# Queries and keys of a decoder layer projected transposed, split where they are made, and loaded whole by the attention

## The chip, the cores and the metric

The kernel runs on one core of a Trainium2 chip. The core has a matrix engine (TensorE, PE in the profile; its weight loads are PEld), a vector engine (VectorE, DVE), an activation engine (ScalarE, ACT), a general engine (GpSimd, POOL), a queue processor (SyncE, SP), and 16 DMA engines between the device memory and the on-chip memory SBUF. TensorE writes to PSUM, 8 banks of 128 x 512 f32. The metric is the device time of one execution in microseconds (us), the median of three.

## The reference

One step of a hybrid decoder layer, for a prompt of 1024 rows of width 1024 and for 8 samples with 8192 cached positions each. All data is f32. Cut to what matters here:

```python
xn = rmsnorm(x, g_mix)                       # x * rsqrt(mean(x*x) + eps) * g
h = xn @ w_in                                # columns: q 512 | k 512 | v 512 | f 8 | u 512 | z 512
logf = log_sigmoid(h_f + b_f); u = gelu(h_u); z = rmsnorm(gelu(h_z), g_sgu_v)
c = cumsum(logf)                             # forget gates, per head
s = q @ k.T / 8 + c[query] - c[key]          # 8 heads of 64, causal
att = softmax(s) @ v
sgu = u * (causal(w_s) @ z + b_s)            # in chunks of 128 rows
x = x + concat(rmsnorm(att), rmsnorm(sgu)) @ w_o
x = x + cross_attention(x, memory); x = x + conv_ffn(x); y = rmsnorm(x)
```

The samples go through the same layer with paged caches of keys, values and gates. The outputs include y and the prompt's k, v and logf.

## The kernel before

**Precision.** A product of two f32 matrices is made of three matmuls in the engine's faster f32r type: each operand is split into a high part (ACT copies it to f32r) and the residual (DVE subtracts), and `gemm3` (L238) sums high x high, high x low, low x high. `split` (L209) makes the parts, `wload` (L221) loads a weight block and splits it (L212, L213).

**Projections (`p1`, L302).** x comes transposed (`xT`), is multiplied by the norm's gain and split into 16 tiles `xh`, `xl` that stay for all of `p1` (`load_x`, L314). The row factor 1/rms(x) is applied after the matmul. The sums of squares come from x in its row layout: `stats` (L323) loads it once more in 4 MB, 1 MB at a time into the `kv` buffers, and ACT squares and sums (L207); these loads are put behind those of `xT` in SP's queue. Then five column blocks follow: Q, F with U, K, V, Z, each a weight load (`loaded`, L346) and 8 row tiles of 24 matmuls. A row tile lies in PSUM with rows on partitions; `evac` (L382) multiplies by the row factor on ACT and ACT's queue stores it row-major (q_d, o_k, o_v). `by_rows` (L387) runs four tiles at once, weight block by weight block. `gate_rows` (L439) makes the cumulated gates and their residuals and stores them in cq_d and ck_d, with rows of ones beside them.

**Attention (`attention`, L629).** It runs for half 0 (rows 0 to 511, 4 key tiles) and half 1 (8 key tiles), in each over 4 pairs of heads. `load` fetches q, k and v of a pair; `setup` (L646) transposes q and k on TensorE (L649, L672), ACT copies the high parts (L655, L656, L676, L680; in half 1 POOL makes one of the copies, L678), DVE the residuals (L657, L681), and POOL's queue adds the gate rows (L658, L667). The results are the operands of `scores` (L684): queries' high and residual parts stacked over 128 partitions against keys' high parts twice (L696), and queries' high parts with 4 gate rows against keys' residuals with 4 gate rows (L698). Row maximum on DVE (L701), exponential on ACT (L706), transposes (`turn`, L724), products with v (`values`, L740). `LD` and `ST` say at which step of a pair the next one's load and setup are written down.

**Beside it.** `pmem` (L590: the memory's keys and values) and `gating` (L535: the spatial gating of one half) are generators that `mix` (L1550) weaves into the attention of half 0 and the cross-attention: each `yield` gives a weight, and the other side runs until the weights balance. `early` (L1581) starts the attention and `pmem` within Z. The samples' step (`decode`, L1123) is woven into everything by `PACE`: gathers of 1 MB of cache by POOL's queue into four `kv` buffers (L1175, L1236), multiplies on DVE or POOL (L1183), sums on DVE (L1187), matmuls with the values (L1242).

**Buffers.** Large tiles `U`: 18 of 128 x 1024 f32. Small tiles `T2`: 7 of 128 x 520. Weight buffers `WRAW`: 4, `kv`: 4. PSUM: 6 banks in turn for most products (`BK`, L128), one `MS`, one `DV`. The order of instructions on each engine is made ahead of time by a list scheduler, which takes the written order as priority.

Of the kernel before, what the change touches and what calls it, by code (L numbers as in the profile page):

```python
# [18 lines left out]
P = 128  # L19
# [39 lines left out]
KP = 2  # L59
PW = 1  # L60
LD = [(0, 1, 0), (0, 0, 0)]
ST = [(0, 1, 1), (0, 1, 1)]
# [12 lines left out]
SB = 2  # L75
# [8 lines left out]
def build(nc, tc, ctx, a, phases=None):  # L84
# [97 lines left out]
    q_d = dram.tile([T, AW], F32, tag="q_d", name="q_d")  # L182
    k_d, v_d = a["o_k"], a["o_v"]
# [3 lines left out]
    cq_d = dram.tile([NH, 4, T], F32, tag="cq_d", name="cq_d")  # L187
    ck_d = dram.tile([NH, 4, T], F32, tag="ck_d", name="ck_d")
# [108 lines left out]
    def newest(e):  # L297

        return next(i for i in reversed(nc.cur_bb.bb.instructions) if i.engine == e)


    def p1(early):  # L302
        rstd = const.tile([P, 8], F32, tag="rstd", name="rstd")
        rstd8 = const.tile([P, 8], F32, tag="rstd8", name="rstd8")
        ssx = sm([P, 8], "ssx", 1)
# [6 lines left out]
        xh, xl = [[U([P, T], F32R) for _ in range(8)] for _ in range(2)]  # L312

        def load_x(kk, hf):  # L314

            raw = WRAW(1024).rearrange("p (k t) -> p k t", t=512)
            c = slice(hf * 512, hf * 512 + 512)
            nc.sync.dma_start(raw, a["xT"][kk * 256 : (kk + 1) * 256, c].rearrange("(k p) t -> p k t", p=P))
            for q in range(2):
                k = kk * 2 + q  # L320
                split(raw[:, q, :], xh[k][:, c], xl[k][:, c], scale=gp[:, G_MIX + k : G_MIX + k + 1])

        def stats(hf):  # L323
            for q in range(2):
                xr = KV().rearrange("p (c d) -> p c d", d=D)
                t0 = hf * 4 + q * 2
                with tc.issue_after(x_in):
                    nc.sync.dma_start(xr, a["x"][t0 * P : (t0 + 2) * P, :].rearrange("(c p) d -> p c d", p=P))
                for i in range(2):
                    ssq_into(ssx[:, t0 + i : t0 + i + 1], xr[:, i, :])  # L330
            c = slice(hf * 4, hf * 4 + 4)
            r = rstd_of(ssx[:, c], D, 4, "r4")
            nc.vector.tensor_copy(rstd[:, c], r)
            nc.vector.tensor_scalar(rstd8[:, c], r, 0.125, None, op0=ALU.mult)
# [11 lines left out]
        def loaded(c0, n, parts, first=False):  # L346

            sp = [(BK(), off, m) for off, m in parts]
            ws = []
            for kk in range(4):  # L350
                if first:
                    load_x(kk, 0)
                w_ = wload(wpair(a["w_in"], kk, c0, n), 2 * n)
                for ps, off, m in sp:
                    sample_mm(ps, w_[2], kk, xsT, m, off)
                ws.append(w_)
                if first and kk == 1:
                    constants()
            return ws, [(ps, m) for ps, off, m in sp]


        ws, sps = loaded(O_Q, 512, [(0, 512)], first=True)
        for kk in range(4):
            load_x(kk, 1)
        x_in = newest(ENG.SP)
# [9 lines left out]
        stats(0)  # L375
        stats(1)
# [5 lines left out]
        def evac(ps, dst, sc, tt):  # L382
            t = T2()
            nc.scalar.activation(t, ps, AF.Copy, scale=sc[:, tt : tt + 1])
            nc.scalar.dma_start(dst[tt * P : (tt + 1) * P, :], t)

# [13 lines left out]
        pss = yield from by_rows(0, ws)  # L400
        for tt in range(8):
            ps = BK() if tt > 3 else pss[tt]
            if tt > 3:
                mm_chunk(tt, ws, ps, 0, 512)
                yield 5.2
            evac(ps, q_d, rstd8, tt)
# [32 lines left out]
        def gate_rows():  # L439
# [3 lines left out]
            for hf in range(2):  # L443
# [11 lines left out]
                for r_, src in ((0, ch), (1, cl)):  # L455
                    nc.sync.dma_start(cq_d[:, r_, s], src.bitcast(F32))
                    nc.sync.dma_start(cq_d[:, 2 + r_, s], one)
                    nc.sync.dma_start(ck_d[:, r_, s], one)
                    ng = T2()[:8]
                    nc.vector.tensor_scalar(ng, src.bitcast(F32), -1.0, None, op0=ALU.mult)  # L460
                    nc.sync.dma_start(ck_d[:, 2 + r_, s], ng)


        for c0, dst in ((O_K, k_d), (O_V, v_d)):
            ws, sps = loaded(c0, 512, [(0, 512)])
            for tt in range(8):
                ps = BK()
                mm_chunk(tt, ws, ps, 0, 512)
# [14 lines left out]
                evac(ps, dst, rstd, tt)  # L483
# [51 lines left out]
    def gating(hf):  # L535
# [6 lines left out]
        for pr_ in range(2):  # L542
            z = U([P, 2, 512])
            u = U([P, 2, 512])
# [3 lines left out]
            nc.sync.dma_start(u, sgu_d[rows, :].rearrange("(c p) d -> p c d", p=P))  # L548
            for i in range(2):
# [3 lines left out]
            yield 1  # L553
# [36 lines left out]
    def pmem():  # L590
        rm = const.tile([P, 2], F32, tag="rm", name="rm")
        ssm = sm([P, 2], "ssm", 1)
        for mt in range(2):
            t = U([P, D])
            nc.sync.dma_start(t, a["mem"][mt * P : (mt + 1) * P, :])
            ssq_into(ssm[:, mt : mt + 1], t)
        r = rstd_of(ssm, D, 2, "r2")
        nc.vector.tensor_copy(rm, r)
        mh, ml = [], []
        for q in range(2):  # L600
            h, l = U([P, 4, 256], F32R), U([P, 4, 256], F32R)
            raw = WRAW(1024).rearrange("p (k m) -> p k m", m=256)
            nc.sync.dma_start(raw, a["memT"][q * 512 : (q + 1) * 512, :].rearrange("(k p) m -> p k m", p=P))
            for k in range(4):
                kk = q * 4 + k
                split(raw[:, k, :], h[:, k, :], l[:, k, :], scale=gp[:, G_MEM + kk : G_MEM + kk + 1])
            mh.append(h)
            ml.append(l)
        yield 0.1
# [19 lines left out]
    def attention(hf, late=None, at=3):  # L629
# [3 lines left out]
        def load(hp):  # L633
            cs = slice(hp * P, (hp + 1) * P)
            qn = T2().rearrange("p (i c) -> p i c", c=P)
            nc.sync.dma_start(qn, q_d[hf * 512 : (hf + 1) * 512, cs].rearrange("(i p) c -> p i c", p=P))
            if hf == 0:
                kvn = U([P, 2 * nk, P])
                kn, vn = kvn[:, :nk, :], kvn[:, nk:, :]
            else:  # L640
                kn, vn = U([P, nk, P]), U([P, nk, P])
            nc.sync.dma_start(kn, k_d[: nk * P, cs].rearrange("(i p) c -> p i c", p=P))
            nc.sync.dma_start(vn, v_d[: nk * P, cs].rearrange("(i p) c -> p i c", p=P))
            return qn, kn, vn

        def setup(hp, qn, kn, vn):  # L646
            tr = (MS, BB, BA)[SB]()
            for i in range(4):
                nc.tensor.transpose(tr[:, i * P : (i + 1) * P], qn[:, i, :], ident)  # L649
            qab, ka, kb = [], [], []  # L650
            for j in range(2):
                h = hp * 2 + j
                rows = slice(64 * j, 64 * j + 64)
                qq = U([P, 2, 512], F32R)
                nc.scalar.activation(qq[0:64, 0, :], tr[rows, :], AF.Copy)  # L655
                nc.scalar.activation(qq[0:64, 1, :], tr[rows, :], AF.Copy)  # L656
                nc.vector.tensor_tensor(qq[64:128, 0, :], tr[rows, :], qq[0:64, 0, :].bitcast(F32), op=ALU.subtract)  # L657
                nc.gpsimd.dma_start(qq[64:68, 1, :], cq_d[h, :, hf * 512 : (hf + 1) * 512])  # L658
                qab.append(qq)
                if hf == 0:  # L660
                    kab = U([P, 2, 512], F32R)
                    ka.append(kab[:, 0, :])
                    kb.append(kab[:, 1, :])
                else:
                    ka.append(U([P, nk * P], F32R))
                    kb.append(U([P, nk * P], F32R))
                nc.gpsimd.dma_start(kb[j][64:68, :], ck_d[h, :, : nk * P])  # L667
            for kh in range(hf + 1):
                yield
                tr = (MS, BB, BA)[SB]()  # L670
                for i in range(4):
                    nc.tensor.transpose(tr[:, i * P : (i + 1) * P], kn[:, kh * 4 + i, :], ident)  # L672
                s = slice(kh * 512, kh * 512 + 512)
                for j in range(2):
                    rows = slice(64 * j, 64 * j + 64)
                    nc.scalar.activation(ka[j][0:64, s], tr[rows, :], AF.Copy)  # L676
                    if KP & 1 << hf:
                        nc.gpsimd.tensor_copy(ka[j][64:128, s], ka[j][0:64, s].bitcast(F32))  # L678
                    else:
                        nc.scalar.activation(ka[j][64:128, s], tr[rows, :], AF.Copy)  # L680
                    nc.vector.tensor_tensor(kb[j][0:64, s], tr[rows, :], ka[j][0:64, s].bitcast(F32), op=ALU.subtract)  # L681
            got.append((qab, ka, kb, vn))

        def scores(qkv, ls, blk, j, ii):  # L684
# [9 lines left out]
            for ch in range(nch):  # L694
                s = BA()[:, :n]
                mmul(s, qab[j][:, 0, i * P : (i + 1) * P], ka[j][:, ch * n : ch * n + n], start=True, stop=False)  # L696
                diag = ch == nch - 1
                mmul(s, qab[j][0:68, 1, i * P : (i + 1) * P], kb[j][0:68, ch * n : ch * n + n], start=False, stop=not diag)  # L698
# [75 lines left out]
        got = []  # L774
        for _ in setup(0, *load(0)):
            pass
        nxt = None
        yield 2
        for hp in range(4):
            for _ in nxt or ():  # L780
                pass
            qkv, nxt = got.pop(), None
            if hp == at and late:
                late()
            for blk in range(2):
# [5 lines left out]
                for j in range(2):  # L791
                    for ii in range(2):
# [20 lines left out]
                        if hp < 3 and (blk, j, ii) == ST[hf]:  # L813
                            nxt = setup(hp + 1, *raw)
                        if nxt:
                            next(nxt, None)
                            yield 1
# [838 lines left out]
    "o_y": (T, D), "o_ys": (NB, D), "o_k": (T, AW), "o_v": (T, AW), "o_lf": (T, NH), "o_mk": (NMEM, D), "o_mv": (NMEM, D),  # L1656
# [81 lines left out]
```

## Time and profile before

| | us |
|---|---|
| median of 3 runs (1969.85 to 1985.79) | 1971.17 |
| the profiled execution | 1971.44 |
| its span, first to last instruction | 1969.6 |
| TensorE busy in it | 1828.8 (93%) |
| DVE, ACT, POOL busy in it | 1395.3, 730.1, 538.0 |

DMA moved 517.05 MB at a mean of 263 GB/s. A line of a timeline reads: start, duration, engine, line of the kernel, operation, output <- input, shapes, and in brackets the idle time of the engine just before and what ended it. In a table of windows each engine has its busy time and, in brackets, its instructions; then come the granted TensorE clock, the share of the DMA engines' time and GB/s. A line of waits reads: who waited <- for whom, us in total, times, longest. Ends of matmuls are modelled, so overlapping matmuls each show more than their distance.

### The profile page before, as it was taken

The page shows a single profiled execution, that of the slowest core. Times are in us where ns is not written, and L with a number is a line of the kernel's source. Part 1 is how long each engine was busy: PE and PEld are TensorE (multiplying, and loading weights), DVE is VectorE, ACT ScalarE, POOL GpSimd, SP SyncE. Part 2 cuts the span into 40 slices and gives each one's busy share as a digit, 9 for nine tenths or more (in the row PEclk, how much of TensorE's full clock was granted, in tenths as well). Part 3 has the DMA queues.
Part 4 walks back from the last instruction along what each step waited for, and adds up shares of the span by engine and source line. Part 5 has one row for each costly group of instructions (what it writes and reads, how often), then busy time and mean ns, then how long its engine had stood idle before and what let it go on. Part 6 is the DMA issues. An engine that isn't in the chain of part 4 may idle for free.

```text
span 1969.6 us, 23939 instructions
## 1 busy us (share of the span) xinstructions
PE 1828.8 (93%) x9159; PEld 1295.1 (66%) x9159; DVE 1395.3 (71%) x1651; ACT 730.1 (37%) x1344; POOL 538.0 (27%) x376
## 2 busy tenths in 40 slices
PE   8899989878899789699999999998999999999997
PEld 5777766556666547477777776666567677667773
DVE  4877466786767798898989999988335549653442
ACT  5332246566723232332432332433324333242331
POOL 1664342342245433323234243333110000000000
PEclk9999989989999989899999999999999999999998
DMA  8766777654487898788778798989664458665755
GB/s 327 257 242 211 290 303 244 244 166 142 161 342 275 325 335 324 249 324 299 291 268 336 271 356 339 374 314 363 232 217 151 150 188 273 233 220 211 271 192 193
DMA packets 160466, 517.05 MB, mean 263 GB/s; under 512 B 20168, under 2 KB 41928, under 8 KB 127584
## 3 DMA queue, kind: packets, MB, share of 16 engines
q0 software_dynamic: 38528, 270.88, 36.5%
q1 hardware_dynamic: 114912, 232.06, 33.8%
q10 hardware_dynamic: 6912, 12.59, 1.7%
q8 instruction: 72, 1.18, 0.2%
q14 instruction: 42, 0.34, 0.0%
HBM read 493.63 MB, written 21.84 MB: 262 GB/s over the span
## 4 chain that ended last, share of the span: by engine, by line
PE 71%; DVE 10%; DMA 9%; issue 5%; ACT 3%; POOL 1%; SPq 0%; ACTq 0%; DVEq 0%; POOLq 0%
PE ba L242 12%; PE ba L243 12%; PE ba L244 12%; PE bb L242 6%; PE bb L243 5%; PE bb L244 5%; PE dv L1242 5%; DVE s L1187 2%; DMA wr<-w_in 2%; DVE kv L1183 2%; DMA kv<-cache_k,kidx 2%; DVE wl L213 1%; PE dv L1485 1%; DMA u<-zg_d 1%; PE ba L1014 1%
## 5 line engine op out<-in xcount | busy, mean ns | idle before, releaser
L212 ACT ACTIVATE wh<-wr 128x1024 fp32r<-128x1024 f32 (+2 forms) x220 | 228.9, 1044 | 506.7 <-PE ba L243 176.5
L213 DVE TENSOR_TENSOR wl<-wr,wh 128x1024 fp32r<-128x1024 f32 (+2 forms) x220 | 268.5, 1231 | 176.7 <-PE ba L244 70.1
L1187 DVE TENSOR_REDUCE s<-kv 128x32 f32<-128x2048 f32 (+1 forms) x139 | 292.1, 2107 | 18.0 <-POOL kv L1183 17.4
L1175 POOL DMA_INDIRECT kv<-cache_k,kidx x128 | 174.3, 1362 | 449.1 <-PE dv L1242 208.4
L1236 POOL DMA_INDIRECT kv<-cache_v,kidx x128 | 182.5, 1426 | 354.3 <-PE dv L1242 224.7
L242 PE MATMUL ba<-wh,u 128*128 128x512 f32 (+1 forms) x674 | 262.4, 391 | 5.5 <-ACT u L212 2.8
L1183 DVE TENSOR_TENSOR kv<-kv,d 128x2048 f32<-128x2048 f32 (+1 forms) x109 | 248.2, 2282 | 24.8 <-DMA kv<-cache_k,kidx 23.7
L243 PE MATMUL ba<-wl,u 128*128 128x512 f32 (+1 forms) x674 | 258.7, 384 | 3.0 <-DVE wl L213 3.0
L244 PE MATMUL ba<-wh,u 128*128 128x512 f32 (+1 forms) x674 | 255.8, 383 | 0.2 <-DVE u L213 0.2
L242 PE MATMUL ba<-u,wh 128*128 128x512 f32 x568 | 227.4, 401 | 0.0
L244 PE MATMUL ba<-u,wl 128*128 128x512 f32 x568 | 225.9, 398 | 0.0
L243 PE MATMUL ba<-u,wh 128*128 128x512 f32 x568 | 225.1, 397 | 0.0
L242 PEld LDWEIGHTS ba<-wh,u 128*128 128x128 f32 x674 | 128.4, 190 | 54.0 <-issue 18.7
L243 PEld LDWEIGHTS ba<-wl,u 128*128 128x128 f32 x674 | 128.1, 190 | 33.9 <-issue 7.1
L244 PEld LDWEIGHTS ba<-wh,u 128*128 128x128 f32 x674 | 127.6, 189 | 28.9 <-issue 3.4
L1242 PE MATMUL dv<-kv,s 128*32 128x512 f32 x1024 | 135.2, 618 | 2.5 <-DMA kv<-cache_v,kidx 2.2
L1183 POOL TENSOR_TENSOR kv<-kv,d 128x2048 f32<-128x2048 f32 (+1 forms) x30 | 119.3, 3985 | 53.5 <-DMA kv<-cache_k,kidx 47.8
L242 PEld LDWEIGHTS ba<-u,wh 128*128 128x128 f32 x568 | 107.3, 189 | 40.4 <-issue 10.1
L244 PEld LDWEIGHTS ba<-u,wl 128*128 128x128 f32 x568 | 107.0, 188 | 34.5 <-issue 10.9
L243 PEld LDWEIGHTS ba<-u,wh 128*128 128x128 f32 x568 | 107.2, 189 | 33.3 <-issue 9.2
L242 PE MATMUL bb<-wh,u 128*128 128x512 f32 (+1 forms) x318 | 124.3, 391 | 1.6 <-ACT u L212 0.9
L243 PE MATMUL bb<-wl,u 128*128 128x512 f32 (+1 forms) x318 | 122.7, 386 | 1.0 <-DVE wl L213 1.0
(394 smaller groups left out, 2947.7 us busy)
## 6 DMA issues: line engine op xcount, KB each, us to landing
wr<-w_up SPq DMA_DIRECT2D x88, 512.0 KB
kv<-w_up SPq DMA_DIRECT2D x22, 1024.0 KB
wr<-w_down SPq DMA_DIRECT2D x40, 512.0 KB
kv<-w_down SPq DMA_DIRECT2D x11, 1024.0 KB
wr<-w_in SPq DMA_DIRECT2D x16, 512.0 KB
wr<-w_o SPq DMA_DIRECT2D x16, 512.0 KB
wr<-w_cq SPq DMA_DIRECT2D x16, 512.0 KB
wr<-w_co SPq DMA_DIRECT2D x16, 512.0 KB
```

The source lines that it names most:

```text
L212: nc.scalar.activation(h, src, AF.Copy)
L213: nc.vector.tensor_tensor(l, src, h.bitcast(F32), op=ALU.subtract)
L242: mmul(out, sh, mh, start=(i == 0), stop=False)
L243: mmul(out, sh, ml, start=False, stop=False)
L244: mmul(out, sl, mh, start=False, stop=(i == n - 1))
L1014: mmul(ps, mv[:, mt, dd * P : (dd + 1) * P], pT[:, mt, :], start=(mt == 0), stop=(mt == 1))
L1175: nc.gpsimd.indirect_dma_start(kv, None, a["cache_k"], off(kidx[:, b, ch : ch + 1]))
L1183: eng.tensor_tensor(kvv[:, i : i + m, :], kvv[:, i : i + m, :], qb.unsqueeze(1).broadcast_to((P, m, 512)), op=ALU.mult)
L1187: nc.vector.tensor_reduce(s[:, ch * 4 + i : ch * 4 + i + m, :].rearrange("p k h -> p (k h)"), kvv[:, i : i + m, :].rearrange("p k (h d) -> ...
L1236: nc.gpsimd.indirect_dma_start(kv, None, a["cache_v"], off(kidx[:, b, ch : ch + 1]))
L1242: mmul(dv[32 * j : 32 * j + 32, :], s[:, ch * 4 : ch * 4 + 4, :].rearrange("p k h -> p (k h)"), kvv[:, j, :], start=(ch == 0), stop=(ch == ...
L1485: mmul(ps[32 * j : 32 * j + 32, q * 256 : (q + 1) * 256].rearrange("p (f c) -> p f c", f=2), xsT[:, k, :], rv[:, k], start=(k < 4), stop=( ...
```

## The change

The queries and keys are projected with the operands exchanged, so that heads lie on partitions and rows on columns; there the row factor, laid out as a row block `rrow`, is multiplied in, the split is made, and the parts are stored as the attention needs them. The attention loads these operands whole; its transposes, copies and residuals are gone. The output k is stored transposed and turned on the host after the run. The sums of squares are made from `xT`: ACT squares, TensorE sums over partitions. `pmem` loads ahead, `gating` waits longer between load and use, and for half 0 uses weight buffers. The core of it:

```diff
+    q1_d, k1_d = (dram.tile([NH, P, T], F32, tag=n_, name=n_) for n_ in ("q1_d", "k1_d"))
+    q2_d, k2_d = (dram.tile([NH, 68, T], F32, tag=n_, name=n_) for n_ in ("q2_d", "k2_d"))
...
+        rrow = U([P, 2, 512])
-        def stats(hf):
...
+        def squares(kk, raw):
             for q in range(2):
+                x2 = T2()
+                nc.scalar.activation(x2, raw[:, q, :], AF.Square)
+                x2s.append((kk * 2 + q, x2))
+        def squares_in():
+            for k, x2 in x2s:
+                j = k % 4
+                mmul(sums[-1][32 * j : 32 * j + 32, :], ones[:, 0:32], x2, start=(k < 4), stop=(k >= 4), tile_position=(0, 32 * j))
+            x2s.clear()
+        def sums_out():
+            t = T2()
+            nc.scalar.activation(t, sums.pop(), AF.Copy)
+            sums_sb.append(t)
+        def factors(hf):
+            t = sums_sb.pop()
+            ps = MS()
+            for i in range(4):
+                mmul(ps[:, i : i + 1], t[:, i * P : (i + 1) * P], ones[:, 0:1], start=True, stop=True)
+            r = rstd_of(ps[:, 0:4], 32 * D, 4, "r4")
+            nc.vector.tensor_copy(rstd[:, hf * 4 : hf * 4 + 4], r)
+        def row_factors(hf):
...
+            mmul(ps, ones, dg, start=True, stop=True)
+            nc.scalar.activation(rrow[:, hf, :], ps, AF.Copy)
...
+        def evac_T(ps, hf, hp, scale, to1, to2, out=None):
+            c = slice(hf * 512, hf * 512 + 512)
+            t, h, l = T2(), T2(512, F32R), T2(512, F32R)
+            nc.vector.scalar_tensor_tensor(t, ps, scale, rrow[:, hf, :], op0=ALU.mult, op1=ALU.mult)
+            split(t, h, l)
+            x, y = (l, h) if out is None else (h, l)
+            heads = lambda dst, r0: dst[2 * hp : 2 * hp + 2, r0 : r0 + 64, c]
+            nc.scalar.dma_start(heads(to1, 0), h.bitcast(F32))
+            nc.scalar.dma_start(heads(to1, 64), x.bitcast(F32))
+            nc.scalar.dma_start(heads(to2, 0), y.bitcast(F32))
+            if out is not None:
+                nc.sync.dma_start(out[hp * P : (hp + 1) * P, c], t)
...
+        pss = yield from by_cols(0, ws, {
+                0: [squares_in, sums_out, partial(second, 0)],
+                1: [partial(second, 1)],
+                2: [partial(factors, 0)],
+                3: [squares_in],
+                4: [partial(second, 2)],
+                5: [partial(row_factors, 0), partial(second, 3)],
+                7: [squares_in, sums_out],
+            })
...
@@ gating
+            z, u = (U([P, 2, 512]) if hf else WRAW(1024).rearrange("p (c d) -> p c d", d=512) for _ in range(2))
...
+            yield 6
...
-            yield 1
+            yield 3
@@ attention
+            q1, q2 = U([P, 2, 512], F32R), U([P, 2, 512], F32R)
+            nc.sync.dma_start(q1.bitcast(F32), q1_d[heads, :, qc].rearrange("h p t -> p h t"))
...
+                for j in range(2):
+                    nc.sync.dma_start(ka[j].bitcast(F32), k1_d[hp * 2 + j, :, kc])
+                    nc.sync.dma_start(kb[j][0:68].bitcast(F32), k2_d[hp * 2 + j, :, kc])
+            nc.sync.dma_start(q2[0:68].bitcast(F32), q2_d[heads, :, qc].rearrange("h p t -> p h t"))
+            vn = (T2() if hf == 0 else U([P, nk * P])).rearrange("p (i c) -> p i c", c=P)
-        def setup(hp, qn, kn, vn):
...
```

`by_cols` is `by_rows` with the operands exchanged, for the four pairs of heads of half 0; the other tiles follow one by one. `second` is `load_x` and `squares` for half 1.

More of the change, by code (lines that the diff above doesn't have):

```diff
@@ L74 @@
 LT = 3
-SB = 2
 KS = 2
@@ L356, in loaded @@
                 ws.append(w_)
+                if first:
+                    squares_in()
+                    squares(*x_)
                 if first and kk == 1:
@@ L772, in drain @@
                 queue.pop(0)()
[L774 to L777, printed above, removed]
+        raw = load(0)
         yield 2
         for hp in range(4):
[L780 to L782 removed]
+            qkv = raw
             if hp == at and late:
```

205 lines of the change are left out of this document (103 added, 102 removed).

## The prediction

> **What bounds the kernel now.** I read the page's busy times first, then a table of windows by stage, then the timeline around the widest hole that it shows, and last the waits and the chain of the two attentions. The table's rows are, in order: the projections Q (to 59.3 us), F with U (to 121), K (to 167), V (to 221), Z (to 276.5), the attention of half 0 (to 396), of half 1 (to 528.6), merge, output projection and cross-attention of half 0 (to 820), and the rest. Its columns are TensorE (PE), its weight loads, VectorE (DVE), ScalarE (ACT), GpSimd (POOL), granted clock, DMA.
>
> ```profile
> span 1969.6 us, 23939 instructions
> PE 1828.8 (93%) x9159; PEld 1295.1 (66%) x9159; DVE 1395.3 (71%) x1651; ACT 730.1 (37%) x1344; POOL 538.0 (27%) x376
> ```
>
> The table by stage:
>
> ```profile
> 0.00:59.30 59.30, 52.03 (x210) 37.28 (x210) 24.00 (x57) 35.56 (x52) 8.18 (x13) 1.00 0.90 327
> 59.30:121.00 61.70, 55.58 (x442) 50.12 (x442) 55.02 (x32) 19.29 (x30) 48.59 (x17) 0.94 0.67 242
> 121.00:167.00 46.00, 42.25 (x181) 32.52 (x180) 37.12 (x33) 11.47 (x18) 20.48 (x9) 0.96 0.66 233
> 167.00:221.00 54.00, 54.00 (x248) 39.93 (x247) 29.52 (x21) 14.66 (x18) 21.42 (x12) 1.00 0.65 229
> 221.00:276.50 55.50, 55.50 (x267) 38.75 (x266) 30.92 (x22) 17.21 (x29) 25.15 (x16) 1.00 0.73 275
> 276.50:396.00 119.50, 98.64 (x520) 71.12 (x520) 79.79 (x138) 71.38 (x160) 42.75 (x38) 0.89 0.76 269
> 396.00:528.60 132.60, 110.00 (x715) 76.66 (x711) 95.61 (x205) 89.14 (x244) 41.73 (x47) 0.93 0.43 144
> ```
>
> TensorE is the bound: 1828.8 of 1969.6 us. V and Z have no hole at all. The attentions lose 119.5 - 98.6 = 20.9 and 132.6 - 110.0 = 22.6 us, and there the clock column falls most, to 0.89 and 0.93. So whatever moves off TensorE or out of its way in the attentions can be gained, and whatever is put into the projections is paid unless it fits beside the matmuls.
>
> ```profile
> 276.96 0.60 PE L672 MATMUL ba<-cp,u 128*128 128x128 f32 x4
> ...
> 281.37 1.06 ACT L212 ACTIVATE wh<-wr 128x1024 fp32r<-128x1024 f32 x1 [3.95 <-DMA wr<-w_ck]
> 282.33 0.57 ACT L655 ACTIVATE u<-ba 64x512 fp32r<-64x512 f32 x1
> ...
> 284.50 0.68 DVE L681 TENSOR_TENSOR u<-ba,u 64x512 fp32r<-64x512 f32 x1 [0.40 <-ACT u L680]
> ...
> 284.52 0.47 PE L696 MATMUL ba<-u,u 128*128 128x128 f32 x1 [6.96 <-ACT u L680]
> ```
>
> Here half 0's attention begins. TensorE has transposed the first queries and keys at 276.3 to 277.6 and has nothing until 284.52: the copies that build its operands (L655, L676, L680) stand on ACT behind a weight split that waits for w_ck. After it the matmuls start 0.43 us apart until 291.5, where they are 0.23 apart in Z.
>
> The waits of TensorE in half 1's attention:
>
> ```profile
> PE ba L696 <- ACT wr L706: 7.4, 6, 2.7
> PE ba L696 <- DVE u L681: 4.1, 3, 2.4
> ...
> PE ba L696 <- DVE u L657: 2.7, 1, 2.7
> ```
>
> L681 and L657 are the residuals made in the setup that the change removes; L706 is the exponential, which stays.
>
> **Projections (Q, K): what is added.** Both keep 192 matmuls of 128x512 with operands swapped, nothing on TensorE. The statistics add 16 matmuls of 128x32 by 512. Four of that form (L254, at 23.37 us) hold up the large ones by 24.35 - 23.05 - 0.23 = 1.07 us. Three of the groups follow such a sample group and add about 0.25 each, three stand alone: 3 x 0.25 + 3 x 1.0 = 3.8 us. The factors add 8 tiny matmuls, about 0.15 each by the transposes below, 1.2 us, and 2 of 128x512 in f32, at most 0.59 each (L1014), 1.2 us. Sum +6.2 us, on the path, since the only wait of TensorE in Q is the first, 7.3 us for w_in. The factors' power is on POOL; behind a 4.6 us multiply there it delays the first evacuation, which two free PSUM banks, 11 us of matmuls, cover.
>
> ACT: 8 squares of 128x1024 (L207, 1.06 us) become 16 of 128x512 (0.63): 8.5 against 10.1 us. But they now stand between the first x and w splits, 2 x 0.63 = 1.3 us per pair; ACT waited 1.5 us for DMA at 12.5 and 1.4 us at 18.1, which hides two of the four; I take +1 (0 to +5, all four late). The evacuations: 16 ACT copies (L384, 0.69) become 16 x (DVE 0.74, as L1061; ACT 0.59; DVE 0.69, as L213) and three or four DMA issues for one on ACT's queue (0.33 each, 32 more: 10.6 us over Q and K, where ACT is 60% and 25% busy); K's output goes out on SP's queue, 8 issues of 0.4 us among weight loads that wait for tiles themselves. DVE gets 8 x 1.43 = 11.4 us in each of Q (24.0 of 59.3 busy) and K (37.1 of 46 busy). In K that makes 48.5 of 46 us; six PSUM banks let TensorE run some 4 tiles of 5.5 us = 22 us ahead and V leaves DVE 24.5 us idle, so I take 0 for it. If that cover were gone it costs the excess, 2.5 us.
>
> Here the row and a rule meet. At 60.47 us two DVE multiplies (L1183) take 13.29 us beside two on POOL (11.95); alone one takes 2.28. The removed residuals read PSUM once and never exceeded 0.70 us; the new ones read two SBUF tiles, like L213, whose largest is 5.58. The Trainium skill (SBUF — State Buffer, Who interferes with whom) says that a DVE instruction with two SBUF inputs and a GpSimd instruction that reads SBUF lock each other out. By the row I charge nothing, by the rule a mean half of POOL's 4.6 us multiply for each of K's 8, 18 us of DVE, which by the 22 us above is just still covered; it would make the sum 0 to 17 us worse.
>
> Removed there: 4 MB of x. POOL's first three cache gathers stood behind it (first at 32.4 us, the fourth at 50.9, waiting for ACT's squares), and their multiplies then fell together at 60 to 74 us; TensorE stood 6.1 us in F, 5.1 of it for a sample sum behind them. The gathers can now start earlier: I take -2 (-6 to 0). Earlier gathers also run beside the first x and w loads, included in the +5 above. Traffic: Q writes 6.3 MB for 2.1, K 8.4 for 2.1, in windows of 0.90 and 0.66 DMA; what late landings would cost is rival three. Stage sum: +6.2 + 1 - 2 = +5 us (0 to +20; the upper end is rival three's beginning).
>
> **Attention 0.** Removed: 32 transposes at 0.15 us (0.60 for four): -4.8. The hole at the start: operands now come by DMA into buffers that Z's last 22 us free one after another (x's tiles), in a stretch with DMA at 0.73, so scores can follow Z at once. The first exponentials still stand behind the ACT split that ends at 282.4, so of 6.96 us of hole and 7 x 0.46 = 3.2 us of slow matmuls I take -6 (0 to -10). Of the other 13 us of holes, the wait on gating's L550 (3.1 us) is covered by work spread between its loads and its use: -3 (0 to -3). The later setups' ACT and DVE work (24 copies of 0.59, 12 residuals of 0.69) I count as -2, the largest wait on it being 0.9 (0 to -6). Against it, vn takes one more of 7 small tiles through two head pairs: +1 (0 to +4). The loads grow from 3.1 to 7.3 MB, 4.2 MB at 385 GB/s (the highest here) = 11 us of DMA in 119.5 us at 0.76: 0.85, hidden. Stage sum: -15 (+4 to -24).
>
> **Attention 1.** 48 transposes: -7.2. POOL loses 16 casts of 0.61 and 16 small DMAs, SP's queue gets eight larger loads per pair for three, with DMA at 0.43 and 6.3 MB more: 16 us in 132.6, hidden. In the chain of waits of this window the setup's residuals and copies stand for 4.8 + 1.4 + 2.1 + 1.5 + 0.7 = 10.5 us and the small ck DMA for 3.5: 14 us. Where they go, the exponential after the row maximum (ACT on L704: 15.7 us of waits) is late next, so I take half, -7 (0 to -14). Stage sum: -14 (0 to -21).
>
> **Later.** gating(1) keeps its 64 matmuls, most of which move to the end of the cross-attention, where TensorE waits 11.0 us at 803 (L929 on L920): 0 (-6 to +6).
>
> **Sum.** 5 - 15 - 14 + 0 = -24 us. The profiled execution took 1971.4 us (span 1969.6 and 1.8 around it), 0.3 above the median 1971.17, so nothing is corrected: 1947.5 us.
>
> **The rivals.** One: the first hole stays, because w_ck still comes late and ACT stands before it. For it speaks that 281.37 is a DMA's time, against it that TensorE has scores to do. Without the -6: -18, 1953 us. Two: the attentions' chain closes over what was removed; row maxima, exponentials and the decode's 2.3 us DVE steps set the pace. For it speaks L706 at the head of the waits, against it that ACT and DVE are both relieved. Attention 1 gives nothing and attention 0 only transposes and hole: 5 - 11 = -6, 1965 us. Three, the other side: the small tiles starve Q and K. Each evacuation holds three of the 7 until its DMAs have landed, so two are under way, one per (landing + 2.1)/2 us, against 5.5 us of matmuls per tile. A q_d write stood 3.3 us in the chain; w_in took 22.4 us to land at 26 to 48 us with DMA at 0.95. K's traffic, 233 + 6.3 MB in 46 us = 370 GB/s, is near the highest. At 17 us of landing each stage loses 8 x (9.6 - 5.5) - 22 = 11 us and the gain is nearly gone; from 20 us it is 22 us each, -24 + 44 = +20: 1991 us. Against it: x's 4 MB are gone from Q's window.
>
> **How the numbers follow.** Chances: forecast 0.48 (its own range 1934 to 1958), rival one 0.12, two 0.18, three 0.22. A measurement of this kernel can tell about 1% from no change, 19.7 us, below 1951.5 and above 1990.9. Faster takes 0.41 of the forecast and 0.03 of rival one: 0.44. Slower is 0.20 of rival three. The rest, 0.36, is within 1%. Low 1930: the lower ends of all stages together are 0 - 24 - 21 - 6 = -51, 1920, and the last 10 us would need all of them at once. High 1992, rival three at 20 us of landing.
>
> **What would show it.** Right: no L649 or L672 rows, the first score within 2 us of Z's last matmul, no slow matmuls after it, the attentions at about 105 and 118 us, Z ending at about 281. Wrong: a score still waiting after 281 (one); an attention 1 above 128 us with L706 unchanged (two); TensorE holes in Q, F or K with a DVE evacuation waiting for a DMA (three). An end of Z beyond 295 us would make the prediction wrong.

## The result and the profile after

The changed kernel takes 2178.0 us (median of 4 runs, 2175.2 to 2184.2), the kernel before on the same chip 1974.4. The ratio is 1.103, with a 95% interval of 1.099 to 1.106: 10% slower, where the prediction had 1947.5 us and a range up to 1992.

The page of the changed kernel: its span, TensorE's busy time, and some rows of the span in 40 slices of 54 us.

```profile
span 2173.4 us, 23795 instructions
...
PE 1856.4 (85%) x9131; PEld 1293.3 (60%) x9131; DVE 1393.1 (64%) x1641; ACT 696.9 (32%) x1284; POOL 538.7 (25%) x328
...
PE   8335754696958899896999999989989999999998
...
PEclk9657886898978999997999999999999999999999
DMA  6323424487866697896987987899875347667754
```

TensorE has hardly more to do (1856.4 against 1828.8 us) and yet drops from 93% to 85% of the span. The gap lies in the first 8 slices; from the second of them on the DMA engines are at 0.2 to 0.4, and the granted clock, which falls where TensorE has holes, is at 0.5 to 0.8. So no engine and no bandwidth is full: something waits.

The table by stage, as in the prediction, with bounds fitted to this run: to Q's first evacuation, Q's evacuations, F and U, K's evacuations, V and Z to the first score, both attentions, the rest.

```profile
0.00:60.00 60.00, 50.83 (x191) 28.62 (x192) 35.11 (x54) 29.46 (x46) 18.29 (x15) 0.97 0.67 236
60.00:200.00 140.00, 46.63 (x207) 34.55 (x206) 32.81 (x34) 14.31 (x22) 15.81 (x9) 0.62 0.30 109
200.00:250.00 50.00, 50.00 (x361) 45.77 (x360) 29.33 (x25) 17.27 (x26) 19.71 (x8) 0.99 0.53 184
250.00:405.00 155.00, 69.97 (x258) 49.93 (x257) 46.17 (x49) 13.23 (x19) 15.63 (x8) 0.70 0.33 115
405.00:492.00 87.00, 83.00 (x386) 58.45 (x384) 56.32 (x42) 24.60 (x41) 41.77 (x23) 0.98 0.80 286
492.00:745.00 253.00, 192.78 (x1125) 132.32 (x1123) 149.80 (x295) 122.41 (x329) 60.78 (x39) 0.88 0.70 234
745.00:2173.40 1428.40, 1363.23 (x6614) 943.66 (x6613) 1043.54 (x1147) 475.65 (x804) 366.68 (x227) 0.98 0.74 275
```

The two stages of the new evacuations last 140 and 155 us and leave TensorE idle for 93 and 85 of them. The first score starts at 491.9 us, 207 later than before (284.5). That is the whole loss: from the first score to the last it is 253 us against 244, and from there on 1428 against 1441.

The chain of waits inside Q, 146 to 191 us, in order of time (start, duration, what), its pieces of 0.6 us and more. ACTq is ACT's queue, the time in which ACT issues a DMA.

```profile
146.60 4.07 ACTq L428
150.77 8.36 ACTq L427
159.24 0.90 issue
160.15 0.63 ACT t L210
160.79 4.75 ACTq L426
165.58 10.63 ACTq L428
176.30 4.94 ACTq L427
181.29 0.64 ACT t L210
181.95 4.27 ACTq L426
186.26 5.01 ACTq L428
```

The issues of the three stores (L426 to L428) are the path. ACT's work on a tile, the copy that makes the high part (L210), takes 0.63 us between them. The same by line: q's and k's stores at the third of them, with min/median/max in ns, and below who waited for it (us in total, times).

```profile
L428 ACTq DMA_DIRECT2D q_d<-t x8: 496/5206/10628, 64.8 to 186.3; - x8
L428 ACTq DMA_DIRECT2D k_d<-t x8: 500/4084/9637, 252.1 to 402.9; - x8
...
  ACT t L210: 96.3, 7
```

In the kernel before, the store of q:

```profile
L385 ACTq DMA_DIRECT2D q_d<-t x8: 326/327/458, 39.6 to 60.2; - x8
```

Both store 256 KB from a tile of 128 x 512. The old one writes 128 rows to consecutive rows; the new one writes two heads of 64 rows with a gap between them, so its destination has 2 as its outermost size. Counted packet by packet in the trace, ACT's queue runs exactly two packets at a time during 85% of its busy time between 60 and 160 us and moves 48.9 GB/s while it is busy; in the kernel before it runs 16 or more at a time in 12% of its busy time and moves 166 GB/s (36 to 62 us). At 48.9 GB/s the 768 KB of a tile take 16.1 us, and the eight tiles of a stage 129 us, of the 140 and 155 us that the two stages last. The Trainium skill states this (DMA: Bandwidth & Descriptors, Why a DMA increments its semaphore by 16 and not by 1): a DMA is dealt to the largest number of engines, up to 16, that divides the slowest dimension of both sides. The trace agrees for 2 here; by that rule the 68-row loads of q2 and k2 get 4, and where those loads run, SP's queue shows four packets at a time more often than any other number (24% of its busy time at 600 to 745 us).

### The profile page after: what moved, and what is told of

It is laid out like the page before. It is cut to its first block, busy times and chain, and to the rows that moved or that the text cites. A ratio compares the mean times of both kernels' runs of the same rounds, so it can differ in the third digit from the quotient of the medians.

```text
span 2173.4 us, 23795 instructions
## 1 busy us (share of the span) xinstructions
PE 1856.4 (85%) x9131; PEld 1293.3 (60%) x9131; DVE 1393.1 (64%) x1641; ACT 696.9 (32%) x1284; POOL 538.7 (25%) x328
## 4 chain that ended last, share of the span: by engine, by line
PE 53%; DMA 12%; issue 10%; DVE 7%; ACTq 5%; POOL 3%; ACT 2%; SPq 0%; POOLq 0%; DVEq 0%
PE ba L240 9%; PE ba L241 9%; PE ba L242 9%; PE bb L240 4%; PE bb L241 4%; PE bb L242 4%; PE dv L1306 4%; DMA k_d<-t 3%; DMA kv<-cache_k,kidx 3%; ACTq L428 2%; DMA kv<-cache_v,kidx 2%; ACTq L427 2%; POOL kv L1300 2%; DVE s L1251 1%; DVE wl L211 1%
## 5 line engine op out<-in xcount | busy, mean ns | idle before, releaser
L210 ACT ACTIVATE wh<-wr 128x1024 fp32r<-128x1024 f32 (+2 forms) x220 | 228.6, 1043 | 513.1 <-PE ba L241 158.8
L1300 POOL DMA_INDIRECT kv<-cache_v,kidx x128 | 205.0, 1601 | 373.6 <-PE dv L1306 161.4
L240 PE MATMUL ba<-wh,u 128*128 128x512 f32 (+1 forms) x620 | 243.4, 394 | 37.8 <-ACT wh L210 25.5
L1247 DVE TENSOR_TENSOR kv<-kv,d 128x2048 f32<-128x2048 f32 (+1 forms) x108 | 236.1, 2190 | 32.3 <-DMA kv<-cache_k,kidx 32.3
L240 PE MATMUL ba<-u,wh 128*128 128x512 f32 x608 | 244.0, 402 | 0.0
L241 PE MATMUL ba<-u,wh 128*128 128x512 f32 x608 | 241.7, 398 | 0.3 <-DVE u L214 0.3
L242 PE MATMUL ba<-u,wl 128*128 128x512 f32 x608 | 240.7, 396 | 0.0
L241 PE MATMUL ba<-wl,u 128*128 128x512 f32 (+1 forms) x620 | 239.8, 388 | 0.8 <-DVE wl L211 0.7
L242 PE MATMUL ba<-wh,u 128*128 128x512 f32 (+1 forms) x620 | 237.4, 388 | 0.0
L240 PEld LDWEIGHTS ba<-wh,u 128*128 128x128 f32 x620 | 120.1, 194 | 81.4 <-ACT wh L210 26.0
L240 PE MATMUL bb<-wh,u 128*128 128x512 f32 (+1 forms) x276 | 109.1, 395 | 49.0 <-ACT wh L210 26.1
L240 PE MATMUL bb<-u,wh 128*128 128x512 f32 x320 | 130.6, 408 | 18.9 <-DVE t L421 17.9
L240 PEld LDWEIGHTS ba<-u,wh 128*128 128x128 f32 x608 | 114.8, 189 | 44.6 <-issue 15.2
L242 PEld LDWEIGHTS ba<-wh,u 128*128 128x128 f32 x620 | 119.9, 194 | 33.4 <-issue 10.0
L241 PEld LDWEIGHTS ba<-u,wh 128*128 128x128 f32 x608 | 114.8, 189 | 35.0 <-issue 9.8
```

Source lines behind the costliest of these rows:

```text
L210: nc.scalar.activation(h, src, AF.Copy)
L240: mmul(out, sh, mh, start=(i == 0), stop=False)
L241: mmul(out, sh, ml, start=False, stop=False)
L242: mmul(out, sl, mh, start=False, stop=(i == n - 1))
L1247: eng.tensor_tensor(kvv[:, i : i + m, :], kvv[:, i : i + m, :], qb.unsqueeze(1).broadcast_to((P, m, 512)), op=ALU.mult)
L1300: nc.gpsimd.indirect_dma_start(kv, None, a["cache_v"], off(kidx[:, b, ch : ch + 1]))
```

## The experiments

Twelve kernels ran. First and last score are starts of TensorE's first and last score matmul; "rest" is from there to the end of the span.

| kernel | median us | ratio to before (95%) | first score | last score | rest |
|---|---|---|---|---|---|
| before (its page) | 1971.2 | | 284.5 | 528.6 | 1441.0 |
| changed | 2178.0 | 1.103 (1.099 to 1.106) | 491.9 | 744.8 | 1428.6 |
| e1: stores cut per head | 2025.4 | 1.022 (1.017 to 1.027) | 318.4 | 587.8 | 1436.1 |
| e2: stores issued by SP | 2173.7, one run | | 476.6 | 739.9 | 1431.9 |
| e3: e1, loads cut | 1997.1 | 1.010 (1.006 to 1.015) | 317.8 | 564.7 | 1427.9 |
| e4: before, 2 blocks | 1987.1 | 1.005 (1.003 to 1.007) | 306.1 | 549.4 | 1434.1 |
| e5: whole rows | 1986.3 | 1.005 (1.003 to 1.008) | 300.3 | 554.7 | 1431.1 |
| e6: e5, half 1 late | 1966.9 | 0.996 (0.994 to 0.999) | 300.6 | 523.5 | 1441.0 |
| e7: e5, statistics from x | 1991.3 | 1.008 (1.005 to 1.012) | 305.3 | 552.9 | 1425.0 |
| e8: e5, squares in f32r | 1976.4 | 1.000 (0.998 to 1.002) | 300.1 | 557.8 | 1414.8 |
| e9: together | 1959.4 | 0.993 (0.990 to 0.996) | 299.8 | 526.3 | 1429.8 |
| e10: before, half 1 late | 1961.5 | 0.994 (0.992 to 0.996) | 287.5 | 532.0 | 1423.0 |
| e11: e7, half 1 late | 1965.6 | 0.996 (0.994 to 0.999) | 307.5 | 520.3 | 1434.6 |
| e12: before, 8 blocks | 1986.1 | 1.005 (1.002 to 1.008) | 287.2 | 538.8 | 1438.1 |

**e1: each store cut per head.**

```diff
-            nc.scalar.dma_start(heads(to1, 0), h.bitcast(F32))
-            nc.scalar.dma_start(heads(to1, 64), x.bitcast(F32))
-            nc.scalar.dma_start(heads(to2, 0), y.bitcast(F32))
+            for j in range(2):
+                src = slice(64 * j, 64 * j + 64)
+                nc.scalar.dma_start(to1[2 * hp + j, 0:64, c], h[src].bitcast(F32))
+                nc.scalar.dma_start(to1[2 * hp + j, 64:128, c], x[src].bitcast(F32))
+                nc.scalar.dma_start(to2[2 * hp + j, 0:64, c], y[src].bitcast(F32))
```

> The changed kernel with each of its three stores per tile cut in two, one per head (64 rows of 512): the same bytes, twice the issues. Theory A (a store whose outermost dimension is the 2 heads runs on 2 of the 16 DMA engines, 48 GB/s, so 256 KB take 5.2 us and three per tile 15.7 us against 5.5 us of matmuls): the stores spread out, an issue on ACT's queue falls from 5 us to below 0.6, Q and K lose their holes, 1940 to 1990 us. Theory B (too many bytes and too many issues for ACT's queue, or too few small tiles): 2178 us or more.

Same bytes, twice the issues, 153 us less. The first of the three lines, by source line:

```profile
L427 ACTq DMA_DIRECT2D q_d<-t x16: 452/608/989, 62.7 to 105.5; - x16
L427 ACTq DMA_DIRECT2D k_d<-t x16: 452/538/1697, 165.6 to 226.3; - x16
```

Half the bytes in 0.6 us instead of 5. Bytes and the number of issues are refuted as the cause, and so is the number of small tiles that an evacuation holds, which is three as before. But 2025 us is above the 1940 to 1990 that were expected, so the stores are not all.

**e2: the three stores issued by SP's queue, shape unchanged** (`nc.scalar.dma_start` to `nc.sync.dma_start` in them).

> The changed kernel with the three stores issued by SP instead of ACT, their shape unchanged. If what costs the time is that ACT stands at the issue (its splits wait behind it), the time falls below 2050 us. If the two engines' rate itself is the limit, because the small tiles are held until the stores land and SP's weight loads now stand behind them, it stays above 2100 us and ACT's waits turn into waits for small tiles.

The time stays, although ACT no longer stands at an issue. The wait has moved to the transfers; SP's issues:

```profile
L426 SPq DMA_DIRECT2D q_d<-t x8: 498/4898/8101, 62.0 to 181.4; - x8
```

And the waits of 60 to 250 us:

```profile
DVE t L211 <- DMA q_d<-t: 37.6, 4, 12.8
ACT wh L210 <- DMA wr<-w_in: 31.2, 1, 31.2
```

DVE waits for small tiles whose stores have not landed, and the weight loads stand behind the stores in SP's queue. SP's queue now runs two packets at a time in 81% of its busy time (60 to 160 us). The blocked issue is only how the slow transfer shows; who issues it does not matter here, as far as one run can tell.

**e3: e1, and each 68-row load cut in 64 and 4 rows.**

```diff
-                nc.sync.dma_start(k2[0:68].bitcast(F32), k2_d[heads, :, kc].rearrange("h p t -> p h t"))
+                for r in (slice(0, 64), slice(64, 68)):
+                    nc.sync.dma_start(k2[r].bitcast(F32), k2_d[heads, r, kc].rearrange("h p t -> p h t"))
```

> The kernel with stores per head, and the attention's loads of 68 rows cut into 64 and 4 rows. Theory A for loads (68 rows go to 4 engines, the largest divisor up to 16): the residuals and gate rows land in less than half the time, the attentions shorten by 5 to 20 us against the kernel with stores per head. Theory B (loads are hidden anyway): within 4 us of it.

28 us less, and in the profiles 22.5 between the first score and the last (269.4 to 246.9), more than the 5 to 20 that were expected. The loads of half 1's keys and of q2, not shown here, are cut in the same way. A load of 68 rows costs time although it moves no more than one of 64 and one of 4.

**e4 and e12: the kernel before, with q's stores alone in 2 blocks of 64 rows, or 8 of 16,** each block followed by an unused row so that the blocks cannot be joined. q is loaded back in 2 or 8 pieces.

```diff
-            nc.scalar.dma_start(dst[tt * P : (tt + 1) * P, :], t)
+            if dst is q_d:
+                nc.scalar.dma_start(q_d[2 * tt : 2 * tt + 2, 0:64, :], t)
+            else:
+                nc.scalar.dma_start(dst[tt * P : (tt + 1) * P, :], t)
```

> The kernel before, with only q's 8 stores given an outermost dimension of 2 (blocks of 64 rows at a pitch of 65, the same bytes and issues; the load of q reads the blocks in two DMAs). Theory A: each store runs on 2 engines for 5.2 us instead of below 1.5, packets of ACT's queue come 2 at a time in Q; a store per 5.5 us tile just keeps up, so the time rises by 0 to 15 us. Theory B: nothing to see in the stores, within 3 us of before.

> The kernel before, in which only q's eight stores of 256 KB go to eight blocks of 16 rows with a gap of one row behind each, so that their outermost dimension is 8 (2 with blocks of 64 rows, 128 or 1 block in the kernel before); q is loaded back in eight pieces, which costs SP's queue some 16 x 7 x 0.4 = 45 us of issuing in the attentions. Theory A (as many DMA engines as the outermost size lets it): no more than 8 of a store's packets run at a time, and a store's issue takes about a quarter of the 5.4 us of the two-block kernel, 1.0 to 1.6 us, or less where the queue takes a store before the one ahead has drained. Rival (any store with a gap in its destination is slow, or it is two engines whenever there is more than one block): 5 us again, two packets at a time. The total: 1975 to 1995, by the eight loads more than by the stores.

The stores of e4:

```profile
L386 ACTq DMA_DIRECT2D q_d<-t x8: 495/5421/9103, 39.9 to 82.2; - x8
```

Those of e12:

```profile
L386 ACTq DMA_DIRECT2D q_d<-t x8: 577/588/1152, 39.8 to 59.8; - x8
```

The same 256 KB take 0.33, 0.59 and 5.4 us to issue in 128 rows on end, 8 blocks and 2 blocks, in a kernel that has nothing else of the change. Packet by packet, ACT's queue never runs more than four at a time in e4 (two for 59% of its busy time, 41 GB/s) and never more than ten in e12, eight the commonest number (15%, 110 GB/s). A gap alone is not slow: the size of the outermost dimension is. With eight stores, one per tile, e4 puts the first score 21.6 us later and the total 11 us up; TensorE waits 13.9 us for weight splits that stand on ACT behind the issues. e12's 0.5% is not its stores': the last is issued at 59.8 us (60.2 in the kernel before), the first score comes 2.7 us later, and TensorE waits 10.3 us for its eight-piece loads of q.

**e5: the parts in four arrays of 512 x 1024,** so that a tile needs two stores of 128 rows on end; the attention puts its operands together from loads of 64 rows and 4 gate rows.

```diff
+            nc.scalar.dma_start(to1[hp * P : (hp + 1) * P, c], h.bitcast(F32))
+            nc.scalar.dma_start(to2[hp * P : (hp + 1) * P, c], l.bitcast(F32))
...
+            two = lambda d, c: d[cs, c].rearrange("(h p) t -> p h t", p=64)
+            for r, d in ((slice(0, 64), qh_d), (slice(64, 128), ql_d)):
+                nc.sync.dma_start(q1[r].bitcast(F32), two(d, qc))
```

> The changed kernel, with q and k's high and low parts kept as four arrays of 512 x 1024 in DRAM: each evacuation issues two stores of 128 x 512 instead of three of two heads (or six of one head), and the attention loads the rows that it needs from them in pieces of 64 rows, and the gate's 4 rows from an array of their own. Theory A (a transfer goes to as many DMA engines as its outermost size lets it, and what was left after the stores were cut per head is six issues of 0.6 us on ScalarE's queue and small tiles held by them): K's last evacuation falls from 224 us to 185-205 us, the stores' issues to 0.35 us, the total to 1965-1985. Rival (the stores are no longer what holds the projections; the statistics from x transposed, or the evacuation's VectorE work, are): K's last evacuation stays above 215 us and the total at 1990-2000.

K's last evacuation comes at 204.8 us, inside the expected 185 to 205 though at its end, the issues take 0.33 us, and the total falls by 11 us to just above the expected 1985. (The intervals of e3 and e5 overlap; that K's last evacuation was at 223.9 us in e3 speaks for the gain.)

**e6 and e10: half 1's first loads behind half 0's attention** (`LT = 3` to `LT = 4`), in e5 and in the kernel before. In e3 the chain shows why this was asked, at 420 to 455 us:

```profile
425.54 9.60 DMA u<-k_d
435.15 14.84 DMA u<-wsT
450.01 1.24 DVE u L640
451.29 2.08 PE bb L658 x8
```

Gating's weights (wsT) land 14.8 us behind half 1's keys, and TensorE waits 11.6 us for the product made from them; the DMA engines are at 0.9 and more there, so these loads are not hidden.

> The kernel of whole rows, in which the first loads of half 1's attention are issued behind half 0's attention with its gating, not ahead of gating's loads. Theory: with the loads of half 1 (2.5 MB, 10 us at 400 GB/s) ahead of them on SP's queue, gating's weights and rows came 12 us late in half 0's attention; put behind, TensorE's wait for VectorE's L640-like multiply falls below 3 us, and half 1's attention begins with a wait for its own loads of 8-15 us instead: the total within 5 us of the kernel of whole rows. Rival (the order alone is at fault, not the bytes): 8-12 us faster. Other rival (half 1's start stands bare): 10-20 us slower.

> The kernel before, with the first loads of half 1's attention issued behind half 0's attention as in the two kernels above. There they are 1.25 MB instead of 2.5, and gating's loads waited little. Theory (what the order gave the changed kernel, 19 us, was the price of the larger loads): no faster than before, 0 to +10 us, since half 1's transposes then wait for loads. Rival (the order is a gain of its own): 5 to 15 us faster.

e6 is 19 us faster than e5, more than either reading had; the wait on gating is gone and half 1's start did not pay for it. But e10 is 13.5 us faster than the kernel before too, against the theory: the order is a gain of its own, and only some 6 us of the 19, little more than the intervals can tell, belong to the larger loads. In e10 it appears behind the last score (1441.0 to 1423.0), not where e6 shows it; why is not settled.

**e7, e8 and e11: the statistics.** e7 takes them from x as before. e8 writes the squares as f32r and sums them against f32r ones, so they are rounded first, in products with one 128 x 128 tile of ones instead of four of 128 x 32:

```diff
-                x2 = T2()
+                x2 = T2(512, F32R)
...
-                mmul(sums[-1][32 * j : 32 * j + 32, :], ones[:, 0:32], x2, start=(k < 4), stop=(k >= 4), tile_position=(0, 32 * j))
+                mmul(sums[-1], ones_r, x2, start=(k == 0), stop=(k == 7))
```

> The kernel of whole rows, with the statistics from x as it lies (4 MB loaded, 8 squares of 128 x 1024 with their sums, no statistics on TensorE), as in the kernel before; the rest as changed. My prediction's terms for this part are +6.2 us on TensorE, +1 on ScalarE and -2 for the hole in F: by them this kernel is 5 us faster than the one of whole rows (0 to 10). Rival (the 16 squares in small tiles and the chain behind them delay Q's first evacuation by the 20 us seen: 61 against 39 us): the first evacuation at 40-50 us and the total 10-25 us below the kernel of whole rows. Other rival (4 MB more of loads in the fullest stretch cost more than the matmuls): 5-15 us slower.

> The kernel of whole rows (1986.3 us) with the 16 squares written as f32r tiles and summed against f32r ones, 128 x 128 by 512, for 16 f32 products that stand in the trace as 32 matmuls of 0.59 us. The squares are so rounded to f32r before they are summed. Theory (I priced these products by a sample group, 3.8 us, where the trace has 32 x 0.59 = 18.9 us busy on TensorE): TensorE's busy time falls by about 32 x 0.59 - 16 x 0.28 = 14 us, Q's first evacuation from 61 to 50-56 us, the total by 5 to 15 us. Rival (the loads of w and x set the pace there and TensorE would only wait longer): busy time falls, the total by less than 4 us.

> Statistics from x as it lies, whole rows, half 1's first loads late, and both row factors asked for later (half 0's behind the last of its products, not three products ahead of it, where TensorE waited 16.9 us; half 1's one tile later). Theory (with that wait gone the statistics from x, which take nothing on TensorE, cost less than the f32 ones): 1950-1965 us. Rival (their 4 MB of loads hold up w_in and the gathers, as K's late last evacuation, 210 against 205 us, lets one think): 1965-1975 us.

The 16 products in e5:

```profile
L328 PE MATMUL ms<-t,ones x32: 592/592/1061, 7.2 to 52.9; 128*32 128x512 f32 x32
```

In e8:

```profile
L329 PE MATMUL ms<-t,ones_r x16: 388/395/796, 7.2 to 47.9; 128*128 128x512 f32 x16
```

The f32 products stand as 32 matmuls of 0.59 us, but up to four of them overlap: together they keep TensorE busy for 12.1 us, not for the sum of 18.9 on which e8's expectation rests. The f32r ones keep it busy for 6.45. e8 takes 8.6 us off TensorE's busy time (1832.0 to 1823.4, less than the 14 expected) and 10 us off the total. But the first evacuation comes at 58.2 us, not at 50 to 56, and the first score does not move (300.3 to 300.1): ahead of it TensorE is busy 5.1 us less and idle 4.9 us more. The gain appears behind the last score, so it is not shown to be that of the products. e7 is inconclusive: it is 5 us slower where 5 us faster was expected, with intervals that overlap; TensorE is relieved by 11.5 us, but its row factors come where TensorE waits 16.9 us for them. With that wait down to 5.3 us and half 1's row factors later as well, e11 is at the border between its two expectations (1965) and equals e6 within the intervals: statistics from x and f32 statistics from x transposed cost about the same here.

**e9: e8, half 1 late, and half 1's row factors one tile later.**

> Whole rows, f32r squares, half 1's first loads behind half 0's attention, and half 1's row factors made one tile later, so that TensorE does not wait 8.6 us for their diagonal. Theory: the gains add, 1966.9 - 10 - 5 = 1945 to 1960 us, below the kernel before by 1 %. Rival (the projections' loss is taken back by the later, slower waits of the decode that is interleaved with them): 1960-1970.

1959.4 us is the fastest, 0.7% below the kernel before, at the upper end of what was expected. But e10, the kernel before with the same order, has 0.994 (0.992 to 0.996) against 0.993 (0.990 to 0.996): with its transfers mended, the change itself is worth nothing that these runs can tell.

## Why the prediction was wrong

**The step that failed is the price of the new stores in the projections.** The prediction took "0.33 each" for an issue, the row of a store of 128 rows on end, and carried it to stores in two blocks; and it set their bytes, "Q writes 6.3 MB for 2.1, K 8.4 for 2.1", against the DMA share of the windows, so that the sum has nothing for them. What counted was the shape of each store: the 48 issues of the changed kernel take 216 us of ACT's queue, a median of 4.8 each. That term, 0, measures 153 us (changed kernel to e1), and with the cut into whole rows a further 11 (e3 to e5).

**Rival three** had the place, Q and K, and the sign, at 0.22, but not the law. It let landing times of 17 to 20 us come from crowding, over the number of small tiles. The traces show a rate: two packets at a time, 16.1 us a tile, with the DMA engines at 0.30; and e4 has the same slow stores where an evacuation holds one small tile. Hence 207 us and not 44. The prediction's own test, "An end of Z beyond 295 us would make the prediction wrong", is met by far: Z's last matmul starts at 491.7 us.

**Loads "hidden" in both attentions.** Wrong by 28 us for the 68-row shape (e1 to e3), and by some 6 more for the bytes at the change of halves, where the share of DMA time is near 1 (e6 and e10). I divided the bytes by a whole stage of 119.5 us; they are due at its start and end. (The 385 GB/s called the highest is not: 26 to 48 us of the kernel before moves 412.)

**The statistics, 3.8 us,** were sized by the gaps of a sample group of four. The trace has 12.1 us of busy time for them in e5. The row factors, 1.2 us, cost 11.2 us of waiting in e5 (2.6 and 8.6 us, for DVE's diagonal at L357, which stands behind evacuations that wait for small tiles) and 25.8 in one wait in the changed kernel. DVE's new work was right in its first step (L421), which never exceeded 0.69 us.

**The residuals, the row against the rule.** In the changed kernel none of the sixteen of 128 x 512 exceeds 0.70 us, but there none meets a multiply on POOL. In e5 three start within one, and these three are the slow ones: 4.24, 4.93 and 3.92 us, 11.0 us above the 0.69 of the others. Each ends 0.55 us behind POOL's multiply. So do 20 of the 21 residuals that start within such a multiply in all the runs with these evacuations; the exception is in e7 (0.68 us). Two of e5's, from e5's timelines of POOL and DVE:

```profile
70.76 4.54 POOL L1252 TENSOR_TENSOR kv<-kv,d 128x2048 f32<-128x2048 f32 x1 [6.87 <-DMA kv<-cache_k,kidx]
71.62 4.24 DVE L211 TENSOR_TENSOR t<-t,t 128x512 fp32r<-128x512 f32 x1 [3.16 <-ACT t L210]
...
165.05 4.58 POOL L1252 TENSOR_TENSOR kv<-kv,d 128x2048 f32<-128x2048 f32 x1 [4.74 <-DMA kv<-cache_k,kidx]
166.26 3.92 DVE L211 TENSOR_TENSOR t<-t,t 128x512 fp32r<-128x512 f32 x1 [2.34 <-ACT t L210]
```

So the rule had the mechanism and the row, which charged nothing, did not; the 18 us were too many, since of K's eight one was held, for 3.2 us. The first of the three stands ahead of the diagonal for which TensorE waits 8.6 us. The Trainium skill's lock between DVE and GpSimd (SBUF — State Buffer, Who interferes with whom) fits all three.

**The projections' sum, +5 (0 to +20),** does not hold even with the stores mended. Z's last matmul starts at 276.3 us in the kernel before, at 300.1 in e5 and 299.6 in e9: +24 and +23, again beyond the 295 of the prediction's own test. Up to that matmul TensorE is busy 17.3 us more in e5 and idle 6.4 us more, by the statistics and the row factors above all. F's -2 came: the wait for a sample sum that it stood for, 5.1 us, is 0.7 in e5.

**The attentions, -29 together,** were right in mechanism only with the other order of loads. In e6 they take 222.9 us from first score to last, 21.2 less than before, and the 8 us of hole ahead of the first score are gone: it comes at 300.6, 0.2 us behind Z's last matmul. But the -6 for that hole did not come, because a hole opens behind the first scores instead. There TensorE waits 12.0 us for Z's evacuations on ACT (L621), in the waits of 300 to 430 us:

```profile
PE ba L775 <- ACT t L621: 9.8, 1, 9.8
...
PE ba L240 <- ACT t L621: 2.2, 1, 2.2
```

In e10 the order alone changes this stretch by 0.4 us. With the order of loads that the prediction had, nothing of the gain shows (253 us in the changed kernel, 254.4 in e5), and half 1's exponential is still ahead of scores in the changed kernel:

```profile
PE bb L657 <- DVE u L639: 18.6, 1, 18.6
PE ba L240 <- ACT t L727: 10.0, 1, 10.0
PE ba L770 <- ACT wr L780: 9.3, 5, 5.8
```

The first line is gating, whose -3 became a wait of 18.6 us: its loads are queued behind half 1's. The yields added between load and use do not help a load that is issued late. The upper ends of the two ranges, +4 and 0, allow for transposes that give nothing; with their -4.8 and -7.2 kept, the same terms add up to -1 and -7.

**Later, 0 (-6 to +6).** The rest takes 1428 us against 1441 in the changed kernel, but 1441 in e6, where the attentions gained most. That something is taken back there is not shown. Eight of the kernels do the same 6586 matmuls in this stretch, with 144 of the decode's 1024 matmuls with the values done before it, and it lasts from 1414.8 (e8) to 1441.0 us (the kernel before). It so moves by up to 26 us for reasons that no run isolates, with one profile for each kernel; the gains of e8 and e10 lie in it too.

## What to carry to other kernels

Write down the shape of every new transfer beside its bytes: a store or load whose outermost size is 2 (or 68, which 16 doesn't divide) runs a few packets at a time, whatever the mean DMA share says is free. The Trainium skill has this as a rule (DMA: Bandwidth & Descriptors, Rules for kernel authors): put a multiple of 16, best the 128 partitions, outermost; here it was worth 153 us of 2178. And when a changed kernel is improved by a new order of loads, try that order in the old one before the change is given the credit.

## What was not expected of the hardware

- An issue of a 256 KB store to 2 blocks holds its engine's queue for a median of 4.8 us (up to 15.9), against 0.33 for 128 rows on end; ACT, at 32% of the span, so became the path.
- The cost grows steeply between 8 blocks (0.59 us an issue) and 2 (5.4 us).
- Where TensorE waited for it, the granted clock fell to 0.62 and 0.70 for 140 and 155 us. The 128 x 512 matmuls of L240 took 0.49 and 0.53 us on average between 60 and 200 us, against 0.40 between 405 and 492.
- A residual on DVE with two inputs in SBUF that starts within a POOL multiply ends 0.55 us behind it (20 of 21 in all runs); in e5 that makes it 3.2 to 4.2 us late.
